# Delta rule's triangular inverse: 8x8 blocks and two doublings in place of 16x16 and one, with masks for selections

## The chip, the cores and the metric

The kernel runs on one core of a Trainium2 chip. The metric is the device time of one execution in microseconds (us). The core has five engines with instruction queues of their own, each run strictly in program order: PE (TensorE, matmul), DVE (VectorE), ACT (ScalarE), POOL (GpSimd) and SP (SyncE, which issues most transfers). They wait for one another by semaphores.

## The reference, cut to what matters

A hybrid decoder layer, 1024 tokens of width 1024. One projection feeds a gated delta rule (4 heads of 128) and a differential attention (4 heads); an output projection, then a gated feed-forward layer of 2816 follow. The change touches the delta rule alone. With chunks of tokens it solves a unit lower triangular system per chunk and head:

```
g = jnp.cumsum(chunks(g), axis=-1)
decay = jnp.exp(jnp.where(tril, g[..., :, None] - g[..., None, :], -jnp.inf))
lower = jnp.where(strict, jnp.einsum('bhnid,bhnjd->bhnij', k_beta, k) * decay, 0.0)
sol = lax.linalg.triangular_solve(eye + lower, rhs, left_side=True, lower=True,
                                  unit_diagonal=True)
...
v_new = value_i - jnp.einsum('bhck,bhkv->bhcv', kcd_i, state)      # scan over chunks
state = state * jnp.exp(gl_i)[..., None, None] + jnp.einsum('bhck,bhcv->bhkv', k_i, v_new)
```

The kernel takes chunks of 128 tokens, so there are NT = 8 chunks a head, and it works with the transposed system: `U` holds one 128x128 upper triangular matrix per chunk, side by side in a 128x1024 tile.

## The kernel before, in words

The program has four stretches: loading and normalising (to about 95 us), the four heads of the delta rule with the projections around them (95 to about 350 us), attention and the output projection (to about 760 us), and the feed-forward layer (to the end). The order of the instructions is fixed when the program is built: parts of the program have priorities (the table `PRI`, unchanged here), and a scheduler lays out each engine's queue by them. At run time no engine overtakes anything in its own queue.

In the delta stretch PE's queue is filled up with the matmuls of the projections: `gT` (L422 to L424, three matmuls of 128x512 for one product in split precision) and `pn` (L403 to L406). Between them stand the short matmuls of the heads. For head h the functions are:

- `delta_prep`: loads the cumulated decay as rows (`dec`), takes the exponential `eg`, subtracts the column term `Gc` (DVE L592), masks the triangle (POOL L594), and takes one exponential over 128x1024 (ACT L597). It runs a convolution of four taps for k, q and v (`conv4`: ACT L570, three DVE L573, silu ACT L575), transposes k, q and v on PE (`pk` L611, `pv` L657), and forms `pkk`, `pkq` (L638, L639), `U` (L643) and `dec` (L645).
- `delta_inverse`: cuts the four 32x32 diagonal blocks out of `U` into `Ud` (four POOL selections, L673), inverts their 16x16 diagonal blocks by 15 rounds of a DVE shuffle, multiply and subtract (L684, L685, L687), spreads the result into 32x32 blocks `Zd`, transposes it to `ZdT`, and doubles the block size once with two groups of 32 matmuls of 32x32 (`pv0` L696, `pz0` L702). Two further doublings, to 64 and to 128 (`pv1` L714, `pz` L726, `pv2` L736, `pz2` L741), follow.
- `delta_scan`: eight chunks in sequence, each a chain between PE and DVE: `pP` (PE L754), DVE L756, `pzz` (L758), DVE L762, `pS` (L766), DVE L771. It also evicts on ACT (L763, L776).
- `delta_out`: normalises and gates the output.

The inverse of head h+1 is laid out between the steps of the scan of head h on DVE, and the preparation of one head beside the inverse of the one before. POOL meanwhile also forms `wlo` (L204), the low part of projection weights, from two tiles in SBUF.

## Time and profile before

| | |
|---|---|
| median of 3 runs | 1429.08 us (1425.96 to 1431.47) |
| profiled execution | 1430.1 us, span 1428.4 us |
| PE busy | 1334.5 us, 93% of the span |
| DVE busy | 878.3 us, 61% |
| ACT busy | 611.3 us, 43% |
| POOL busy | 377.0 us, 26% |
| mean granted TensorE clock | 0.975 |

Busy is the time in which an engine had an instruction running; PE's can overlap its own next instruction. The chain of work that ended last consists almost only of PE instructions of the feed-forward layer.

### The profile page before, as it was taken

To read this page: it belongs to the slowest core of one execution; us is meant where nothing else is said; L and a number is where in the kernel's file an instruction comes from. 1 tells how busy PE (TensorE), PEld (TensorE's weight loads), DVE (VectorE), ACT (ScalarE), POOL (GpSimd) and SP (SyncE) were. 2 spreads that over 40 slices of the span, in tenths; PEclk is the share of its full clock that TensorE was granted. 3 is DMA by queue.
4 is the path that set the end of the run, shared out by engine and by line. 5 is a ranking of instruction groups with operands and counts; after the bars stand their busy time and mean duration, and the time that the engine had idled before them with its cause. 6 is when DMAs were issued, how large, how long until landed. Compare 5 with 4: busy or idle time off the path is not lost. (4 is left out here: it accounts for less than half of the span.)

```text
span 1428.4 us, 20608 instructions
## 1 busy us (share of the span) xinstructions
PE 1334.5 (93%) x7927; PEld 1126.6 (79%) x7927; DVE 878.3 (61%) x1745; ACT 611.3 (43%) x1086; POOL 377.0 (26%) x295
## 2 busy tenths in 40 slices
PE   7998898989989998999887999999999989999998
PEld 6876676888989986778665788888888868888887
DVE  5467978886342368867787666666666656334321
ACT  6445454533325365665554444444444435222220
POOL 3044313131242245240022434444333420000000
PEclk8999999999999999999998999999999999999999
DMA  7231112031543267455331222222222247547421
GB/s 225 83 80 35 34 39 75 17 113 66 162 109 116 88 169 192 105 134 162 123 121 29 89 74 89 85 78 89 89 74 82 82 137 243 195 149 229 139 88 59
DMA packets 143393, 155.14 MB, mean 109 GB/s; under 512 B 9279, under 2 KB 114367, under 8 KB 143295
## 3 DMA queue, kind: packets, MB, share of 16 engines
q1 hardware_dynamic: 130815, 144.14, 31.8%
q0 software_dynamic: 11008, 8.39, 3.1%
q8 instruction: 62, 1.02, 0.3%
q10 hardware_dynamic: 1472, 1.29, 0.3%
q14 instruction: 36, 0.29, 0.1%
HBM read 111.32 MB, written 38.29 MB: 105 GB/s over the span
## 5 line engine op out<-in xcount | busy, mean ns | idle before, releaser
L385 PE MATMUL pd<-whi,gl 128*128 128x512 f32 x352 | 137.0, 389 | 0.0
L383 PE MATMUL pd<-whi,gh 128*128 128x512 f32 x352 | 137.0, 389 | 0.0
L384 PE MATMUL pd<-wlo,gh 128*128 128x512 f32 x352 | 137.0, 389 | 0.0
L204 POOL TENSOR_TENSOR wlo<-raw,whi 128x1024 fp32r<-128x1024 f32 x34 | 83.8, 2471 | 194.1 <-PE gT L424 68.2
L1316 POOL TENSOR_TENSOR acc<-acc,acc 128x1024 f32<-128x1024 f32 x22 | 53.6, 2437 | 243.8 <-issue 215.5
L403 PE MATMUL pn<-whi,xn 128*128 128x256 f32 x448 | 116.3, 293 | 0.0
L404 PE MATMUL pn<-whi,xn 128*128 128x256 f32 x448 | 115.4, 291 | 0.0
L1339 ACT ACTIVATE gh<-act 128x1024 fp32r<-128x1024 f32 x42 | 44.6, 1061 | 123.9 <-PE pd L384 100.2
L1340 DVE TENSOR_TENSOR gl<-act,gh 128x1024 fp32r<-128x1024 f32 x42 | 52.0, 1241 | 68.9 <-ACT gh L1339 68.6
L403 PEld LDWEIGHTS pn<-whi,xn 128*128 128x128 f32 x448 | 87.3, 195 | 0.3
L404 PEld LDWEIGHTS pn<-whi,xn 128*128 128x128 f32 x448 | 87.0, 195 | 0.1
L202 ACT ACTIVATE whi<-raw 128x1024 fp32r<-128x1024 f32 x58 | 61.0, 1052 | 52.1 <-issue 18.3
L206 DVE TENSOR_TENSOR wlo<-rx,whi 128x1024 fp32r<-128x1024 f32 x22 | 28.9, 1315 | 82.6 <-ACT whi L202 82.3
L424 PE MATMUL gT<-xn,wlo 128*128 128x512 f32 x192 | 79.3, 413 | 0.0
L1230 PE MATMUL pa<-xT,whi 128*128 128x512 f32 x176 | 70.5, 400 | 9.3 <-ACT xT L1103 5.3
L422 PE MATMUL gT<-xn,whi 128*128 128x512 f32 x192 | 78.8, 410 | 0.0
L423 PE MATMUL gT<-xn,whi 128*128 128x512 f32 x192 | 78.6, 409 | 0.0
L202 ACT ACTIVATE whi<-rx 128x1024 fp32r<-128x1024 f32 x22 | 23.3, 1061 | 127.4 <-POOL rx L1271 127.4
L383 PEld LDWEIGHTS pd<-whi,gh 128*128 128x128 f32 x352 | 66.1, 188 | 13.8
L385 PEld LDWEIGHTS pd<-whi,gl 128*128 128x128 f32 x352 | 66.1, 188 | 13.7
L384 PEld LDWEIGHTS pd<-wlo,gh 128*128 128x128 f32 x352 | 66.1, 188 | 13.6
L206 DVE TENSOR_TENSOR wlo<-raw,whi 128x1024 fp32r<-128x1024 f32 x24 | 29.4, 1225 | 72.3 <-PE pd L384 53.1
(377 smaller groups left out, 3765.9 us busy)
## 6 DMA issues: line engine op xcount, KB each, us to landing
act<-act_dram SPq DMA_DIRECT2D x42, 512.0 KB, 4.5
rw<-in_w_up_dram SPq DMA_DIRECT2D x22, 512.0 KB, 3.8
act_dram<-acc SPq DMA_DIRECT2D x22, 512.0 KB, 2.6
raw<-in_w_down_dram SPq DMA_DIRECT2D x22, 512.0 KB, 4.4
raw<-in_w_in_dram SPq DMA_DIRECT2D x18, 512.0 KB, 4.0
pn_dram<-pn SPq DMA_DIRECT2D x16, 512.0 KB, 3.4
rx<-in_w_up_dram SPq DMA_DIRECT2D x22, 256.0 KB, 2.8
rz<-in_w_up_dram SPq DMA_DIRECT2D x22, 256.0 KB, 3.3
```

Source lines behind the costliest of these rows:

```text
L202: S.activation(hi, raw[:, 0:w], AF.Copy)
L204: G.tensor_tensor(lo, raw[:, 0:w], hi.bitcast(F32), op=ALU.subtract)
L206: V.tensor_tensor(lo, raw[:, 0:w], hi.bitcast(F32), op=ALU.subtract)
L383: PE.matmul(ps, lh, rh, start=first, stop=False)
L384: PE.matmul(ps, lh, rl, start=False, stop=False)
L385: PE.matmul(ps, ll, rh, start=False, stop=last)
L403: PE.matmul(o, xs(xn, 0, kt, a, b), wh, start=kt == 0, stop=False)
L404: PE.matmul(o, xs(xn, 1, kt, a, b), wh, start=False, stop=False)
L422: PE.matmul(o, whi[:, kt, :], xs(x_, 0, kt, *qs), start=kt == 0, stop=False)
L423: PE.matmul(o, whi[:, kt, :], xs(x_, 1, kt, *qs), start=False, stop=False)
L424: PE.matmul(o, wlo[:, kt, :], xs(x_, 0, kt, *qs), start=False, stop=kt == NK - 1)
L1230: PE.matmul(ps, wh[:, ks], xh[k], start=first, stop=False, skip_group_check=not start)
```

## The change

The diff does four things. (1) The column term of the decay goes into the exponential as its bias (`nGc`, the negated `Gc`): the subtraction over 128x1024 goes, and one exponential becomes eight of 128x128, since the bias is one column per chunk. (2) The diagonal 32x32 blocks are copied by ACT without a selection, and multiplied on DVE by constant masks (`s8`, `o8`, `o16`, `m8`), which come in a larger constant table. (3) The blocks that are inverted by rounds are 8x8: 7 rounds over narrower rows in place of 15. (4) From 8 to 16 and from 16 to 32 the pass with `pv0` and `pz0` runs, so twice a head; its first eviction moves from DVE to ACT. The attention mask leaves the early load of constants and is loaded by a transfer of its own.

```diff
--- before.py
+++ after.py
@@ -25,7 +25,9 @@
 NF = FFN // P
 EPS = 1e-6
 LAM_INIT = 0.8 - 0.6 * math.exp(-0.3 * 0)
-C_ID, C_TRI, C_MASK, C_ID16, C_FREQ, C_AB, C_W = 0, 128, 256, 384, 400, 408, 410
+
+C_ID, C_TRI, C_FREQ, C_ID8, C_M8, C_S8, C_O8, C_O16, C_W, C_MASK = 0, 128, 256, 264, 272, 276, 308, 340, 372, 372
+C_ALL = C_MASK + 128
 
 
 GB, WB, RB, LB, JB, CB, SB, OB, LA, S1, S2 = 16, 5, 3, 2, 2, 4, 8, 1, 2, 3, 5
@@ -44,13 +46,17 @@
 
 
 def constants():
-    c = np.zeros((P, C_W), np.float32)
+    c = np.zeros((P, C_ALL), np.float32)
     c[:, C_ID:C_ID + P] = np.eye(P)
     i = np.arange(P)
     c[:, C_TRI:C_TRI + P] = i[:, None] <= i[None, :]
     c[:, C_MASK:C_MASK + P] = np.where(i[None, :] <= i[:, None], 0.0, -1e30)
-    c[:, C_ID16:C_ID16 + 16] = (i % 16)[:, None] == np.arange(16)[None, :]
-    c[:, C_AB:C_AB + 2] = (i // 16 % 2)[:, None] == np.arange(2)[None, :]
+    r, j = (i % 32)[:, None], np.arange(32)[None, :]
+    c[:, C_ID8:C_ID8 + 8] = (i % 8)[:, None] == np.arange(8)[None, :]
+    c[:, C_M8:C_M8 + 4] = r // 8 == np.arange(4)[None, :]
+    c[:, C_S8:C_S8 + 32] = (r // 8 == j // 8) & (r < j)
+    c[:, C_O8:C_O8 + 32] = (r // 16 == j // 16) & (r // 8 < j // 8)
+    c[:, C_O16:C_O16 + 32] = r // 16 < j // 16
     c[:, C_FREQ:C_FREQ + 8] = 500000.0 ** (-np.arange(0, 16, 2) / 16.0)
     return c
 
@@ -150,8 +156,8 @@
     k_sb = cp.tile([P, C_W], F32, name="k_sb")
     ident = k_sb[:, C_ID:C_ID + P]
     tri = k_sb[:, C_TRI:C_TRI + P]
-    id16 = k_sb[:, C_ID16:C_ID16 + 16]
-    halfA, halfB = k_sb[:, C_AB:C_AB + 1], k_sb[:, C_AB + 1:C_AB + 2]
+    id8, m8 = k_sb[:, C_ID8:C_ID8 + 8], k_sb[:, C_M8:C_M8 + 4]
+    s8, o8, o16 = (k_sb[:, a:a + 32] for a in (C_S8, C_O8, C_O16))
 
     warm = small("warm", 1, 1)
     G.memset(warm, 1.0)
@@ -172,7 +178,7 @@
     w1row = gt("w1row")
     xt0 = [load_x(0)]
     nc.scalar.dma_start(w1row, norm1_w.broadcast_to([P, D]))
-    nc.scalar.dma_start(k_sb, cst)
+    nc.scalar.dma_start(k_sb, cst[:, 0:C_W])
     xt0.append(load_x(1))
 
 
@@ -374,7 +380,8 @@
     identb = cp.tile([P, P], BF16, name="identb")
     G.tensor_copy(identb, ident)
     maskb = cp.tile([P, P], BF16, name="maskb")
-    G.tensor_copy(maskb, k_sb[:, C_MASK:C_MASK + P])
+    nc.sync.dma_start(rowsA[:, 640:768], cst[:, C_MASK:C_MASK + P])
+    G.tensor_copy(maskb, rowsA[:, 640:768])
 
 
     dab = cp.tile([P, NT, 8], F32, name="dab")
@@ -544,6 +551,8 @@
     V.tensor_tensor(ekd, Gl, Gc, op=ALU.subtract)
     S.activation(ekd, ekd, AF.Exp)
     S.activation(egl, Gl, AF.Exp)
+    nGc = g32("nGc")
+    V.tensor_scalar(nGc, Gc, -1.0, None, op0=ALU.mult)
 
 
     lamp = tmp(128)
@@ -589,12 +598,12 @@
         with part("d_dec"):
             eg = gt("eg")
             S.activation(eg, dec, AF.Exp)
-            V.tensor_tensor(by_chunk(dec), by_chunk(dec),
-                            Gc[:, h, :].unsqueeze(2).broadcast_to([P, NT, P]), op=ALU.subtract)
             G.affine_select(out=by_chunk(dec), in_=by_chunk(dec),
                             pattern=[[0, NT], [1, P]], base=0, channel_multiplier=-1,
                             compare_op=ALU.is_ge, fill=-1e30)
-            S.activation(dec, dec, AF.Exp)
+            for c in range(NT):
+                cs = slice(c * P, (c + 1) * P)
+                S.activation(dec[:, cs], dec[:, cs], AF.Exp, bias=nGc[:, h, c:c + 1])
         with part("d_k"):
             kT = conv4(4 + h)
         with part("d_q"):
@@ -663,6 +672,7 @@
     def delta_inverse(d):
 
 
+
         inv1, inv2 = gt("inv1"), gt("inv2")
         w4 = [by_chunk(inv1[:, i * 256:(i + 1) * 256], 32) for i in range(4)]
         Ud, Zd, bc, ZdT = w4
@@ -670,38 +680,41 @@
         Uv = by_chunk(d["U"])
         for b in range(4):
             bs = slice(32 * b, 32 * b + 32)
-            G.affine_select(out=Ud[bs], in_=Uv[bs, :, bs],
-                            pattern=[[0, NT], [1, 32]], base=0, channel_multiplier=-1,
-                            compare_op=ALU.is_gt, fill=0.0)
-        U16, Z16, bc16 = (by_chunk(inv2[:, 512 + i * 128:640 + i * 128], 16) for i in range(3))
-        S.activation(U16, Ud[:, :, 0:16], AF.Copy, scale=halfA)
-        V.scalar_tensor_tensor(U16, Ud[:, :, 16:32], halfB, U16, op0=ALU.mult, op1=ALU.add)
-        G.memset(Ud[:, :, 0:16], 0.0)
-        G.tensor_scalar(Ud[:, :, 16:32], Ud[:, :, 16:32], halfA, None, op0=ALU.mult)
-        V.tensor_copy(Z16, id16.unsqueeze(1).broadcast_to([P, NT, 16]))
-        for l in range(15, 0, -1):
-            n = 16 - l
-            V.stream_shuffle(bc16[:, :, 0:n], Z16[:, :, l:16], [l] * 16 + [16 + l] * 16)
-            V.tensor_tensor(bc16[:, :, 0:n], bc16[:, :, 0:n], U16[:, :, l:l + 1].broadcast_to([P, NT, n]),
+            S.activation(Ud[bs], Uv[bs, :, bs], AF.Copy)
+        by_c = lambda m: m.unsqueeze(1).broadcast_to([P, NT, 32])
+        Uo = by_chunk(inv2[:, 512:768], 32)
+        U8, Z8, bc8 = (by_chunk(inv2[:, 768 + i * 64:832 + i * 64], 8) for i in range(3))
+        V.tensor_tensor(bc, Ud, by_c(s8), op=ALU.mult)
+        V.tensor_reduce(U8, bc.rearrange("p c (s j) -> p c j s", j=8), axis=AX.X, op=ALU.add)
+        V.tensor_copy(Z8, id8.unsqueeze(1).broadcast_to([P, NT, 8]))
+        for l in range(7, 0, -1):
+            n = 8 - l
+            V.stream_shuffle(bc8[:, :, 0:n], Z8[:, :, l:8], [8 * (i // 8) + l for i in range(32)])
+            V.tensor_tensor(bc8[:, :, 0:n], bc8[:, :, 0:n], U8[:, :, l:l + 1].broadcast_to([P, NT, n]),
                             op=ALU.mult)
-            V.tensor_tensor(Z16[:, :, l:16], Z16[:, :, l:16], bc16[:, :, 0:n], op=ALU.subtract)
-        S.activation(Zd[:, :, 0:16], Z16, AF.Copy, scale=halfA)
-        V.tensor_scalar(Zd[:, :, 16:32], Z16, halfB, None, op0=ALU.mult)
+            V.tensor_tensor(Z8[:, :, l:8], Z8[:, :, l:8], bc8[:, :, 0:n], op=ALU.subtract)
+        V.tensor_tensor(Zd.rearrange("p c (s j) -> p c s j", j=8),
+                        Z8.unsqueeze(2).broadcast_to([P, NT, 4, 8]),
+                        m8.unsqueeze(1).unsqueeze(3).broadcast_to([P, NT, 4, 8]), op=ALU.mult)
         V.transpose(inv1[:, 768:1024], inv1[:, 256:512])
-
-        pv0 = psS("pv0")
-        for c in range(NT):
-            for b in range(4):
-                bs = slice(32 * b, 32 * b + 32)
-                PE.matmul(pv0[bs, c * 32:c * 32 + 32], Ud[bs, c, :], ZdT[bs, c, :], start=True, stop=True)
-        V.tensor_copy(inv1[:, 512:768], pv0[:, 0:256])
-        pz0 = psS("pz0")
-        for c in range(NT):
-            for b in range(4):
-                bs = slice(32 * b, 32 * b + 32)
-                PE.matmul(pz0[bs, c * 32:c * 32 + 32], bc[bs, c, :], Zd[bs, c, :], start=True, stop=True)
-        V.tensor_tensor(inv1[:, 256:512], inv1[:, 256:512], pz0[:, 0:256], op=ALU.subtract)
-        V.transpose(inv1[:, 768:1024], inv1[:, 256:512])
+        V.tensor_tensor(Uo, Ud, by_c(o8), op=ALU.mult)
+
+        for off in (Uo, Ud):
+            pv0 = psS("pv0")
+            for c in range(NT):
+                for b in range(4):
+                    bs = slice(32 * b, 32 * b + 32)
+                    PE.matmul(pv0[bs, c * 32:c * 32 + 32], off[bs, c, :], ZdT[bs, c, :], start=True, stop=True)
+            S.activation(inv1[:, 512:768], pv0[:, 0:256], AF.Copy)
+            if off is Uo:
+                V.tensor_tensor(Ud, Ud, by_c(o16), op=ALU.mult)
+            pz0 = psS("pz0")
+            for c in range(NT):
+                for b in range(4):
+                    bs = slice(32 * b, 32 * b + 32)
+                    PE.matmul(pz0[bs, c * 32:c * 32 + 32], bc[bs, c, :], Zd[bs, c, :], start=True, stop=True)
+            V.tensor_tensor(inv1[:, 256:512], inv1[:, 256:512], pz0[:, 0:256], op=ALU.subtract)
+            V.transpose(inv1[:, 768:1024], inv1[:, 256:512])
         G.memset(ZT[0:32, :, 32:64], 0.0)
         G.tensor_copy(ZT[0:32, :, 0:32], ZdT[0:32])
         G.tensor_copy(ZT[32:64, :, 32:64], ZdT[32:64])
```

The lines of the changed kernel are shifted: the rounds are L692, L693, L695, `pv0` is L707, `pz0` L715, the transposes `pk` are L620, the convolution is L582 and the silu L584.

DVE's queue, head 0's inverse (tile `inv`) and the convolutions of k and q of head 1 (`acc_1432`, `acc_1438`), before:

```order
L687 TENSOR_TENSOR inv_143_1045<-inv_143_1045 128x8x4
L592 TENSOR_TENSOR dec_1246<-dec_1246,Gc 128x1024
L573 SCALAR_TENSOR_TENSOR acc_1432<-pT_1248,dcw,acc_1432 128x1023
L573 SCALAR_TENSOR_TENSOR acc_1438<-pT_1307,dcw,acc_1438 128x1023
L573 SCALAR_TENSOR_TENSOR acc_1432<-pT_1248,dcw,acc_1432 128x1022
L573 SCALAR_TENSOR_TENSOR acc_1438<-pT_1307,dcw,acc_1438 128x1022
L573 SCALAR_TENSOR_TENSOR acc_1432<-pT_1248,dcw,acc_1432 128x1021
L573 SCALAR_TENSOR_TENSOR acc_1438<-pT_1307,dcw,acc_1438 128x1021
L684 STREAM_SHUFFLE inv_143_1045<-inv_143_1045 128x8x5
```

and with the change (`acc_1491` and `acc_1497` are the same convolutions):

```order
L692 STREAM_SHUFFLE inv_143_1054<-inv_143_1054 128x8x5
...
L695 TENSOR_TENSOR inv_143_1054<-inv_143_1054 128x8x5
L692 STREAM_SHUFFLE inv_143_1054<-inv_143_1054 128x8x6
...
L695 TENSOR_TENSOR inv_143_1054<-inv_143_1054 128x8x6
L692 STREAM_SHUFFLE inv_143_1054<-inv_143_1054 128x8x7
L693 TENSOR_TENSOR inv_143_1054<-inv_143_1054 128x8x7
L695 TENSOR_TENSOR inv_143_1054<-inv_143_1054 128x8x7
L696 TENSOR_TENSOR inv_142_1053<-inv_143_1054,k_sb 128x256
L582 SCALAR_TENSOR_TENSOR acc_1491<-pT_1301,dcw,acc_1491 128x1023
L582 SCALAR_TENSOR_TENSOR acc_1497<-pT_1360,dcw,acc_1497 128x1023
L582 SCALAR_TENSOR_TENSOR acc_1491<-pT_1301,dcw,acc_1491 128x1022
```

All seven rounds and the multiply by `m8` (L696) now stand ahead of the convolutions; before, four rounds and the subtraction L592 did.

PE's queue at the transposes of k of head 1, before (`gT` are projection matmuls):

```order
L423 MATMUL gT_1972<-xn_141,whi_1942 128x512
L611 MATMUL pk_1447<-k_sb,acc_1432 128x128 x4
L611 MATMUL pk_1457<-k_sb,acc_1432 128x128 x4
L424 MATMUL gT_1972<-xn_140,wlo_1943 128x512
...
L422 MATMUL gT_1972<-xn_140,whi_1942 128x512
L611 MATMUL pk_1467<-k_sb,acc_1438 128x128 x4
...
L611 MATMUL pk_1476<-k_sb,acc_1438 128x128 x4
```

and with the change:

```order
L429 MATMUL gT_2075<-xn_140,whi_2045 128x512
L707 MATMUL pv_144_1086<-inv_142_1053,inv_143_1054 32x32 x27
L620 MATMUL pk_1506<-k_sb,acc_1491 128x128 x4
L620 MATMUL pk_1516<-k_sb,acc_1491 128x128 x4
L707 MATMUL pv_144_1086<-inv_142_1053,inv_143_1054 32x32 x5
L430 MATMUL gT_2075<-xn_141,whi_2045 128x512
...
L620 MATMUL pk_1526<-k_sb,acc_1497 128x128 x4
L715 MATMUL pz_145_1121<-inv_142_1053 32x32 x9
L620 MATMUL pk_1535<-k_sb,acc_1497 128x128 x4
```

Head 0's first doubling now stands on both sides of these transposes; 27 of its 32 matmuls are ahead of them. Between `pv` of head 0 and these transposes there are 57 `gT` matmuls, where there were 51.

PE's queue at the second doubling of head 0, which the kernel before has not; `pv_1605` and `pv_1611` are the transposes of v of head 1:

```order
L431 MATMUL gT_2134<-xn_140,wlo_2105 128x512
L666 MATMUL pv_1605<-k_sb,acc_1599 128x128 x2
L707 MATMUL pv_146_1156<-inv_142_1053 32x32 x32
L666 MATMUL pv_1605<-k_sb,acc_1599 128x128 x2
L666 MATMUL pv_1611<-k_sb,acc_1599 128x128 x2
L715 MATMUL pz_147_1190<-inv_142_1053 32x32 x4
L666 MATMUL pv_1611<-k_sb,acc_1599 128x128
L715 MATMUL pz_147_1190<-inv_142_1053 32x32
L666 MATMUL pv_1611<-k_sb,acc_1599 128x128
L715 MATMUL pz_147_1190<-inv_142_1053 32x32 x27
L429 MATMUL gT_2134<-xn_140,whi_2104 128x512
```

Before, the two groups of 32 of the only pass stood at this place with three `gT` matmuls and more between them; now there are four 128x128 transposes.

## Rows read from the trace of the kernel before

**Rows 1.** windows: busy us of each engine (x instructions), TensorE clock, DMA share, GB/s

```profile
95.00:350.00 255.00, 224.47 (x2145) 188.79 (x2144) 209.77 (x585) 117.09 (x284) 70.96 (x57) 0.96 0.17 53
760.00:1430.00 670.00, 654.52 (x2856) 536.98 (x2856) 365.32 (x373) 245.57 (x262) 157.38 (x104) 0.99 0.35 112
125.00:150.00 25.00, 20.00 (x92) 16.11 (x91) 23.65 (x60) 14.26 (x30) 10.95 (x10) 0.96 0.12 37
150.00:175.00 25.00, 21.56 (x262) 17.09 (x261) 23.09 (x82) 8.93 (x28) 10.46 (x11) 0.98 0.09 23
```

**Rows 2.** waits of PE, 95 to 350 us: total, times, longest

```profile
PE pk L611 <- ACT acc L575: 8.3, 2, 5.1
PE pzz L758 <- DVE s L756: 5.3, 3, 2.1
PE pS L766 <- DVE s L762: 4.0, 4, 1.7
PE pkq L639 <- DVE dec L645: 3.2, 2, 1.7
PE pP L754 <- DVE s L771: 3.1, 2, 1.6
PE pv L657 <- ACT acc L575: 3.0, 2, 1.8
```

**Rows 3.** groups on DVE, 95 to 360 us: busy, mean ns, idle before

```profile
L687 DVE TENSOR_TENSOR inv<-inv 128x8 f32<-128x8 f32 (+14 forms) x60 | 20.9, 348 | 1.2
L685 DVE TENSOR_TENSOR inv<-inv 128x8 f32<-128x8 f32 (+14 forms) x60 | 17.6, 294 | 1.5
L684 DVE STREAM_SHUFFLE inv<-inv 128x8 f32<-128x8 f32 (+14 forms) x60 | 14.2, 236 | 0.0
...
L592 DVE TENSOR_TENSOR dec<-dec,Gc 128x1024 f32<-128x1024 f32 x4 | 4.9, 1220 | 8.9 <-ACT eg L591 8.9
...
L703 DVE TENSOR_TENSOR inv<-inv,pz 128x256 f32<-128x256 f32 x4 | 1.7, 414 | 0.0
```

**Rows 4.** groups on POOL, 95 to 360 us

```profile
L673 POOL TENSOR_SCALAR_AFFINE_SELECT inv<-U 32x256 f32<-32x256 f32 x16 | 14.8, 923 | 0.7
```

**Rows 5.** timeline of DVE at 264.9 us: start, length

```profile
264.94 2.33 DVE L687 TENSOR_TENSOR inv<-inv 128x120 f32<-128x120 f32 x1
```

**Rows 6.** timeline of POOL at the same place

```profile
264.73 2.40 POOL L204 TENSOR_TENSOR wlo<-raw,whi 128x1024 fp32r<-128x1024 f32 x1 [9.01 <-PE gT L423]
```

**Rows 7.** timeline of PE around the first block of 32x32 matmuls

```profile
169.03 0.40 PE L422 MATMUL gT<-xn,whi 128*128 128x512 f32 x1
169.26 0.39 PE L423 MATMUL gT<-xn,whi 128*128 128x512 f32 x1
169.73 0.75 PE L696 MATMUL pv<-inv 32*32 32x32 f32 x64
170.41 0.50 PE L424 MATMUL gT<-xn,wlo 128*128 128x512 f32 x1
```

**Rows 8.** timeline of ACT before the first head's values

```profile
129.58 0.40 ACT L677 ACTIVATE inv<-inv,k_sb 128x128 f32<-128x128 f32 x1 [9.04 <-POOL inv L673]
129.89 1.04 ACT L575 ACTIVATE acc<-acc 128x1024 f32<-128x1024 f32 x1
```

**Rows 9.** timeline of DVE around the second head's convolutions

```profile
134.23 1.22 DVE L592 TENSOR_TENSOR dec<-dec,Gc 128x1024 f32<-128x1024 f32 x1
135.37 10.23 DVE L573 SCALAR_TENSOR_TENSOR acc<-pT,dcw,acc 128x1023 f32<-128x1023 f32 x6
```

**Rows 10.** windows around a pair of PE waits, columns as in rows 1

```profile
240.80:246.80 6.00, 2.52 (x12) 1.55 (x11) 5.71 (x18) 2.77 (x4) 5.17 (x6) 1.00 0.11 38
246.80:250.20 3.40, 3.40 (x17) 3.12 (x16) 2.20 (x13) 0.73 (x2) 0.00 (x0) 0.50 0.58 154
```

**Rows 11.** groups on ACT, 95 to 360 us

```profile
L763 ACT ACTIVATE s<-pzz,cj 128x128 f32<-128x128 f32 x28 | 10.1, 361 | 31.0 <-DVE s L762 30.4 <-PE pzz L758 0.6
L718 ACT ACTIVATE U<-inv 32x256 f32<-32x256 f32 x16 | 6.6, 414 | 6.4 <-DVE inv L685 4.2 <-DVE inv L703 2.0
```


## The prediction

> **What bounds the kernel now.** I read the busy time by stretch first. The feed-forward stretch is PE's: 654.5 of 670 us, clock 0.99, and the change does not reach it [rows 1]. Attention isn't touched either, apart from a mask that arrives long before it is used. So the change can only act between 95 and 350 us. There PE is busy for 224.5 of 255 us, which leaves 30.5 us of idle time, and DVE is busy for 209.8. In two windows DVE has hardly a gap, 23.65 and 23.09 of 25 us, while PE stands 5.0 and 3.4 us [rows 1]. The second view is what PE waits for there [rows 2]. The six groups sum to 26.7 us, and all but the first head's 5.1 us for its silu depend on DVE's or ACT's queue in the heads. The stretch is therefore PE work with holes that DVE's queue makes: time is saved by closing holes, and lost by giving PE more to do. Since the projection matmuls that fill PE have to run anyway, each us added to PE's work or to its holes moves the end by about one us.
>
> A third view shows how some holes arise. A multiply and subtract of a round takes about 0.3 us, but this one takes 2.33 us [rows 5], and POOL's subtraction over two tiles in SBUF runs from 264.73 to 267.13 [rows 6]: the DVE instruction ends when POOL's does. The scan's L762 stands behind it, PE's pS behind that, and this is the 1.7 us in the group of pS. The three waits of pzz (5.3 us) and the two of pP (3.1 us) [rows 2] look the same in the timeline: a copy or a round's multiply of about 2 us under POOL work, five times. Such collisions make 5.3 + 3.1 + 1.7 = 10.1 us of the holes.
> The Trainium skill says so too (Trainium Architecture — The Big Picture, "What this means for kernel authors"): DVE and GpSimd share a port pair by an exclusive lock. By that rule the new mask multiplies, with two SBUF inputs each, are as exposed as the rounds were; that is the fourth case below.
>
> **The change part by part.**
>
> *Work on DVE.* A round costs 0.348 + 0.294 + 0.236 = 0.88 us on the mean [rows 3], so eight fewer are 7.0 us a head. The subtraction gives back 1.22 us [rows 3], the eviction and the small merging instructions about 1 us. Added are four multiplies over 128x256, one reduction of that size to 128x64, one more subtraction and one more transpose: seven at about 0.41 us, the price of L703, which has the same shape [rows 3], makes 2.9 us. Net: about -6.3 us a head, -25 us in all, of 209.8. POOL loses its 16 selections, 14.8 us [rows 4]. ACT gains, per head, four copies of 0.41 and two evictions like them, and eight exponentials of 0.36 each, 2.9 us, in place of a single one over the same elements [rows 11]; it was busy for 117 of 255 us, so I cost this at nothing. What covers it is ACT's idle time; where an exponential stands before an eviction of the scan it can hold it by 0.36 us.
>
> *PE's own work: +6.8 us.* A block of 32 matmuls of 32x32 is 64 records in 0.75 us [rows 7]. From L423 at 169.26 to the next gT at 170.41 are 1.15 us where two neighbours are 0.23 apart, so it displaces 0.92 us. Two more blocks a head are eight: 6.0 us by the block, 7.4 by the displacement. I take 6.8.
> The Trainium skill (TensorE: Matmul & The Clock Gate, "Back-to-back issue gap") gives for such short matmuls a floor of about 25 ns, or about 62 ns where the sequencer decodes each in software. By 62 ns the 256 matmuls would cost 15.9 us and the sum below would come out 9 us higher; the row, 0.75 us for 32, is 23 ns each, and it decides.
>
> *Waiting inside the second pass: +1.0 us.* pz0 needs pv0's eviction and pv1 a subtraction and a transpose. Before, three gT matmuls (0.7 us) and more cover each step. Now the four 128x128 transposes of v, or four short pn, cover the second eviction: about 0.55 us against an eviction of 0.41 (as L718) [rows 11] and the handing over. I take 0.25 us a head; bounds 0 and 0.6 a head, 2.4.
>
> *First head's values: -0.7 us.* ACT's queue stands 9.04 us for POOL's selections, and the silu behind it starts at 129.89 [rows 8]. Without them it starts when the convolution ends, by the timeline about 0.7 us earlier, and pv's 1.8 us [rows 2] shrinks by that. Bounds 0 and -1.8.
>
> *k of head 1: +1.3 us.* PE's wait there is 8.3 - 5.1 = 3.2 us [rows 2]. The convolutions start at 135.37, right behind L592 [rows 9]. With the change, all the rounds and four mask multiplies are ahead of them: three more rounds (2.1 us, being narrow), four multiplies and a reduction (2.0 us), less L592 (1.22), less a merge and its wait (0.8). They start about 2.1 us later. Against that, six convolution steps take 10.23 us [rows 9] with POOL's selection and a wlo over them, and part of this goes. PE arrives later as well, by six gT at 0.23 less the 0.7 won just before: 0.7 us. The 27 matmuls of pv0 ahead of pk wait for a transpose that stands behind the convolutions, but are through when the silu of k is. The wait grows by 0.6 to 1.9 us.
>
> *Preparation of head 1: -1.5 us.* Eleven rounds that stood among its steps on DVE are gone. Two waits, 1.7 us in the group of pkq and 3.0 - 1.8 = 1.2 us in that of pv beyond the first head's [rows 2], hang on that queue; I take a bit over half. Bounds 0 and -2.9.
>
> *Collisions: -5 us of 10.1.* Of the five in pzz and pP and the one in pS, three hit rounds 12, 13 and 15, which no longer exist (the largest is rows 5). The others hit a copy or a round that stays. Per head the DVE instructions between SBUF tiles in the inverse fall from 33 to some 21, but wlo also moves on POOL, whose selections no longer hold it up. By the count a third goes, 3.4 us; at best all. I take half.
>
> *Other waits of the scans: -1.7 us.* pS waits 4.0 - 1.7 = 2.3 us beyond that collision, 0.7 of it behind L592. I take 0.7 and 1.0 of the rest.
>
> *Clock: -1.7 us.* Behind two close waits (PE busy for 2.52 of 6 us) the granted clock is 0.50, the 1.2 GHz level, for 3.4 us [rows 10]. That costs 1.7 us each time. Behind the k of head 1 it falls too, as it will again; of the two falls in the scans I count one gone.
>
> *Sum:* 6.8 + 1.0 - 0.7 + 1.3 - 1.5 - 5.0 - 1.7 - 1.7 = -1.5 us. From the profiled 1430.1 us this gives 1428.6. The median of the runs lies 1.0 us below that profiled execution, so the forecast is **1427.5 us**. The best ends of all terms (6.0 for PE, no wait in the second pass, all collisions and clock falls gone) give about -14 us; the worst (7.4, 2.4, 1.9 and no relief) about +12 us.
>
> **The rivals.** 0.5%, 7.1 us, is about what a measurement of this kernel tells from no change.
>
> *Holes close (faster).* DVE loses 12% of its work in the stretch, and the holes come from a queue that is nearly full, so most vanish together: -9 for collisions, -2.9, -3.4 for the clock, -2.3 for pS, -0.7, against 6.8 + 0.6: -11 us, 1418 us. For it: DVE at 23 of 25 us where PE waits. Against it: each hole is a single late instruction, not a queue that never catches up, as PE's full windows between them show.
>
> *PE pays, relief fails at k (slower).* The convolutions of head 1 slip by more than the 2.1 us counted: the decay's selection no longer waits for a subtraction and falls on the rounds ahead of them, and one multiply of about 2 us is added. The wait of pk becomes about 7 us (+3.9), and each later step of head 1 starts as late; with 6.8 + 1.0 and only 3.4 of relief the sum is +8 us, 1437 us. It decides from about 5 us of growth at this place, or when relief stays under 1 us. For it: the queue rows of DVE.
>
> *The masks collide as the rounds did.* The holes stay in number and size: 6.8 + 1.0 + 1.3 - 0.7 - 1.5 - 1.7 = +5 us, 1434 us, within 0.5%.
>
> **How the numbers follow.** Forecast as summed 0.40 (its own range 1421 to 1434); holes close 0.29; pays at k 0.18; masks collide 0.13. The forecast case leaves a little on either side: faster by over 0.5% 0.33, within 0.5% 0.45, slower 0.22. The range reaches from the middle of the faster case's lower half to just past the slower case: 1415 to 1439 us.
>
> **What the profile after would show.** PE's busy time in the delta stretch up by 6 to 7.5 us, with 256 more matmuls of 32x32; DVE's down by about 25 us, POOL's by about 15 to 18. PE's wait for k of head 1 near 4.5 us. Waits of pzz, pP and pS below 10 us together; if they are above 14, the collision term is wrong, if under 3, the faster case holds. The second pz0 of each head waiting for ACT by under 0.6 us; over 1 us there, the eviction's place in ACT's queue was misjudged. The feed-forward stretch must have the same length; if it has not, the cause lies outside this reading.

## The result: slower by 1.2%

The changed kernel takes 1445.02 us (median of 4 runs, 1441.69 to 1451.49) against 1427.52 us of the kernel before on the same chips: a ratio over the executions of 1.0118, 95% interval 1.0088 to 1.0148 (the medians alone give 1.0123). That lies above the forecast range of 1415 to 1439 us. The profiled execution has a span of 1442.4 us.

First, where the time came. The first matmul of attention's scores starts at 410.8 us before and at 426.0 us with the change, 15.2 us later, and what follows it is as long as before (1017.6 and 1016.4 us). Of the 15.2 us, 0.9 are there already ahead of the delta stretch: the short matmuls `pg` (the sums of the decay), which stand in front of it, start at 85.45 us before and at 86.34 with the change. The rest lies where the change was made. A window from 95 us to that matmul, of the kernel before (busy us of PE, PEld, DVE, ACT and POOL with their instructions, then the granted clock, DMA share, GB/s):

```profile
95.00:410.80 315.80, 284.41 (x2623) 246.73 (x2622) 230.10 (x646) 138.08 (x323) 89.49 (x72) 0.97 0.24 72
```

and of the changed kernel, with the stretches of [rows 1]:

```profile
95.00:426.00 331.00, 302.71 (x3138) 259.24 (x3137) 209.83 (x530) 150.91 (x367) 70.46 (x48) 0.95 0.23 69
95.00:350.00 255.00, 228.58 (x2479) 188.48 (x2478) 183.73 (x462) 128.65 (x326) 51.23 (x31) 0.94 0.16 48
760.00:1430.00 670.00, 651.41 (x2846) 534.53 (x2846) 372.24 (x383) 252.15 (x272) 164.76 (x109) 0.99 0.34 109
```

DVE fell by 26.0 us between 95 and 350 us (209.8 to 183.7), and POOL by 19.7. But the changed kernel has done less of its work by 350 us; over the same work, up to attention, DVE fell by 20.3 us (230.1 to 209.8) and POOL by 19.0. PE's idle time up to attention fell too, from 315.8 - 284.4 = 31.4 to 331.0 - 302.7 = 28.3 us. But PE's busy time rose by 18.3 us where 6.8 was expected. Busy time contains the clock: the parts of it that ran at a granted clock of 0.50 (1.2 GHz) are 17.4 us before and 29.7 us after, and half of that is lost time, 8.7 and 14.8 us, if the same work takes twice as long at that clock (an estimate). What is left is PE's work at the full clock: 275.7 and 287.9 us. So the 15.2 us are 12.2 of work, 6.1 of clock and -3.1 of idle time. This split is the measure for every experiment below; I call its parts idle, clock and work.

At 95 us the two kernels are not equally far, so the work is counted from the first `pg` as well:

```profile
85.45:410.79 325.34, 293.95 (x2666) 254.61 (x2665) 232.40 (x651) 142.08 (x330) 91.88 (x73) 0.97 0.25 73
86.34:426.04 339.70, 311.41 (x3178) 266.43 (x3177) 212.25 (x536) 154.96 (x374) 72.90 (x49) 0.95 0.24 70
```

By these the work is 293.95 - 8.7 = 285.3 and 311.41 - 14.8 = 296.6 us, 11.3 more. Idle and clock are the same from either start.

The waits of PE in the changed kernel (us in total, times, longest), 95 to 365 us, to be held against [rows 2]:

```profile
PE omT L814 <- DVE acc L808: 5.4, 3, 3.6
PE pk L620 <- ACT acc L584: 4.4, 1, 4.4
PE pv L666 <- ACT acc L584: 3.4, 2, 2.2
PE pS L779 <- DVE s L775: 3.4, 2, 2.5
PE pv L707 <- DVE inv L699: 3.0, 1, 3.0
PE pkq L648 <- DVE dec L654: 1.8, 1, 1.8
PE pzz L771 <- DVE U L756: 1.2, 1, 1.2
...
PE pz L715 <- ACT inv L708: 0.6, 1, 0.6
```

The collisions in the scans went away as hoped: pzz from 5.3 to 1.2, pP from 4.4 (3.1 and 1.3) to nothing. The 3.0 us of pv0 take the place of the second head's wait for k, since 27 matmuls of pv0 stand ahead of it. New are the waits of omT, the transposes of the gated output (5.4 us), and a longer one of pv. On DVE, 95 to 370 us, as in [rows 3]:

```profile
L695 DVE TENSOR_TENSOR inv<-inv 128x8 f32<-128x8 f32 (+6 forms) x28 | 10.3, 369 | 0.6
...
L693 DVE TENSOR_TENSOR inv<-inv 128x8 f32<-128x8 f32 (+6 forms) x28 | 8.7, 311 | 0.7
...
L692 DVE STREAM_SHUFFLE inv<-inv 128x8 f32<-128x8 f32 (+6 forms) x28 | 5.7, 203 | 0.0
...
L716 DVE TENSOR_TENSOR inv<-inv,pz 128x256 f32<-128x256 f32 x8 | 3.3, 414 | 1.7 <-PE pz L715 1.7
...
L688 DVE TENSOR_REDUCE inv<-inv 128x64 f32<-128x256 f32 x4 | 2.5, 620 | 0.0
...
L687 DVE TENSOR_TENSOR inv<-inv,k_sb 128x256 f32<-128x256 f32 x4 | 1.6, 410 | 0.0
```

The masks (L687) and the subtraction (L716) cost 0.41 us as estimated, the reduction 0.62.

**How PE's work grew.** PE in the last head's second pass (start, length, instructions, idle time before):

```profile
336.96 0.75 PE L707 MATMUL pv<-inv 32*32 32x32 f32 x64 [0.17 <-DVE inv L717]
...
338.94 0.26 PE L715 MATMUL pz<-inv 32*32 32x32 f32 x6 [0.56 <-ACT inv L708]
342.79 0.48 PE L814 MATMUL omT<-k_sb,acc 128*128 128x128 f32 x1 [3.60 <-DVE acc L808]
343.20 0.33 PE L715 MATMUL pz<-inv 32*32 32x32 f32 x8
343.46 0.47 PE L814 MATMUL omT<-k_sb,acc 128*128 128x128 f32 x1
343.86 0.42 PE L715 MATMUL pz<-inv 32*32 32x32 f32 x10
```

After pv0, PE waits 0.56 us for ACT's eviction and then 3.60 us for omT, because the scheduler has put the 8 transposes of the gated output between the pieces of pz0. From there, 8 to 10 records of 32x32 and one transpose alternate, each at twice the length or more that it has in a group. Part of that is the clock, which is at its lower level from 341.85 us on (the test strip below tells the two apart):

```profile
336.30:341.80 5.50, 2.17 (x79) 1.60 (x77) 5.33 (x9) 1.82 (x4) 4.66 (x2) 1.00 0.06 16
341.90:352.00 10.10, 9.21 (x92) 6.97 (x93) 4.68 (x14) 2.73 (x6) 0.78 (x2) 0.50 0.21 86
```

In the 5.5 us ahead of the fall PE was busy for 2.17. The wait itself is a collision once more, at a new place. DVE's and POOL's timelines there:

```profile
336.83 1.94 DVE L191 TENSOR_TENSOR rto<-rto,ms 128x8 f32<-128x8 f32 x1
338.81 2.26 DVE L192 SCALAR_TENSOR_TENSOR ro<-rto,ro 128x8 f32<-128x8 f32 x1
...
341.30 0.17 DVE L191 TENSOR_TENSOR rto<-rto,ms 128x8 f32<-128x8 f32 x1
...
342.38 0.88 DVE L808 SCALAR_TENSOR_TENSOR acc<-acc,ro,szh 128x128 f32<-128x128 f32 x3
```

```profile
336.38 4.66 POOL L804 TENSOR_TENSOR szh<-szh,dnw 128x1024 f32<-128x1024 f32 x2 [9.87 <-ACT szh L803]
```

Two instructions of 128x8 elements, which take 0.17 us a little later, take 1.94 and 2.26 us while POOL multiplies two SBUF tiles (4.66 us for two); the gating L808 starts at 342.38.

### The profile page after: what moved, and what is told of

The parts are those of the page before. It is cut to its first block, busy times and chain, and to the rows that moved or that the text cites. A ratio compares the mean times of both kernels' runs of the same rounds, so it can differ in the third digit from the quotient of the medians.

```text
span 1442.4 us, 21544 instructions
## 1 busy us (share of the span) xinstructions
PE 1351.2 (94%) x8439; PEld 1137.5 (79%) x8439; DVE 858.7 (60%) x1630; ACT 624.5 (43%) x1130; POOL 357.0 (25%) x271
## 3 DMA queue, kind: packets, MB, share of 16 engines
q1 hardware_dynamic: 130959, 144.21, 31.4%
## 5 line engine op out<-in xcount | busy, mean ns | idle before, releaser
L208 ACT ACTIVATE whi<-raw 128x1024 fp32r<-128x1024 f32 x58 | 61.0, 1052 | 50.3 <-issue 18.3
L391 PEld LDWEIGHTS pd<-wlo,gh 128*128 128x128 f32 x352 | 66.1, 188 | 13.7
L392 PEld LDWEIGHTS pd<-whi,gl 128*128 128x128 f32 x352 | 66.1, 188 | 13.6
L413 PE MATMUL pn<-wlo,xn 128*128 128x256 f32 x448 | 71.5, 293 | 2.0 <-POOL wlo L210 2.0
```

The source lines that it names most:

```text
L208: S.activation(hi, raw[:, 0:w], AF.Copy)
L391: PE.matmul(ps, lh, rl, start=False, stop=False)
L392: PE.matmul(ps, ll, rh, start=False, stop=last)
L413: PE.matmul(o, xs(xn, 0, kt, a, b), wf(kt)[1], start=False, stop=kt == NK - 1)
```

## The experiments

Sixteen kernels ran. Each edit stands as a short diff against the kernel named in its expectation. The table has what was measured: the ratio to the kernel before with its 95% interval, and the parts from 95 us to attention's first score matmul, in us. "From pg" is the work counted from the first `pg`, which starts between 83.4 and 88.3 us in these kernels, so that all but the second pass is the same work in all of them (out_later has 17 short projection matmuls more in it, about 2 us, and three others 2 or 3). "Changes" counts, in PE's instructions from there to attention, the places at which a 32x32 matmul stands next to one of a larger tile. mix_cost, the test strip, is the kernel before up to there.

| kernel | ratio (95%) | idle | clock | work | from pg | changes |
|---|---|---|---|---|---|---|
| before | 1 | 31.4 | 8.7 | 275.7 | 285.3 | 46 |
| mix_cost | | 30.9 | 5.9 | 279.4 | 286.2 | 46 |
| changed | 1.0118 (1.0088, 1.0148) | 28.3 | 14.8 | 287.9 | 296.6 | 120 |
| one_pass | 1.0003 (0.9991, 1.0014) | 25.4 | 15.0 | 276.1 | 284.9 | 52 |
| two_passes | 1.0172 (1.0155, 1.0189) | 35.1 | 15.4 | 285.4 | 296.3 | 90 |
| seven_rounds | 0.9998 (0.9980, 1.0016) | 31.4 | 9.4 | 274.9 | 285.5 | 52 |
| bias_alone | 1.0020 (1.0000, 1.0041) | 30.6 | 11.3 | 274.8 | 286.0 | 46 |
| masks_no_bias | 1.0006 (0.9983, 1.0029) | 31.0 | 10.6 | 274.6 | 284.7 | 46 |
| masks_16 | 0.9946 (0.9929, 0.9963) | 26.0 | 10.3 | 272.7 | 284.2 | 44 |
| masks_16_dve | 0.9938 (0.9917, 0.9959) | 25.3 | 7.7 | 274.6 | 285.6 | 46 |
| before_inv_earlier | 1.0015 (0.9998, 1.0031) | 33.1 | 8.6 | 275.1 | 285.8 | 46 |
| inv_earlier | 1.0102 (1.0082, 1.0121) | 34.9 | 11.7 | 282.3 | 292.4 | 74 |
| inv_a_little | 1.0052 (1.0032, 1.0073) | 27.1 | 13.6 | 283.9 | 293.0 | 84 |
| out_later | 1.0094 (1.0064, 1.0123) | 30.3 | 14.2 | 284.9 | 295.1 | 78 |
| omt_later | 1.0040 (1.0018, 1.0062) | 28.7 | 12.7 | 282.8 | 293.3 | 74 |
| evict_dve | 1.0016 (1.0002, 1.0030) | 26.3 | 10.0 | 284.3 | 294.7 | 96 |
| evict_dve_inv | 1.0115 (1.0093, 1.0138) | 36.4 | 16.7 | 280.4 | 291.6 | 74 |
| evict_dve_omt | 1.0102 (1.0070, 1.0135) | 33.5 | 19.8 | 279.8 | 290.9 | 70 |

The ratios are over several executions, the parts of the one that was profiled; for bias_alone that one took 1428.19 us where the median is 1433.04. before and mix_cost show what parts of one queue differ by: 3 us of clock, 1 of work from pg. The nine rows with one pass all have 284.2 to 286.2 us of work from pg, so this column is the firm one; differences of 3 us in the clock column are not.

**Is it the second pass?** (one_pass, two_passes)

```diff
 one_pass, of the changed kernel
-        for off in (Uo, Ud):
+        for off in (Uo,):
 two_passes, of the kernel before: pv0, eviction, pz0, subtraction, transpose
+        for _ in range(2):
```

> The changed kernel without its second doubling (the pass from 16 to 32 is left out, so the blocks stay incomplete). Theory A, the second pass is what costs: its 32x32 matmuls, their mixing with 128x128 transposes on PE and the falls of the clock behind it make about 17 us, and the relief on DVE is worth a few us; 1422 to 1428 us. Theory B, the pass costs only the 6.8 us of its matmuls and the rest lies in the order around the convolutions of k of the second head: 1436 to 1440 us.

> The kernel before with its one doubling pass run a second time on the same blocks (the result is spoilt; nothing else changes). Theory A, a pass costs 10 us or more where pz0 stands between the transposes omT (it does in heads 1 to 3 here, 4 or 5 pieces): 1437 to 1444 us. Theory B, a pass costs the time of its block of matmuls, 6.8 us, and a little for the wait: 1434 to 1436 us.

Without the second pass the changed kernel takes 1426.98 us, the time of the kernel before; with a second pass the kernel before takes 1451.95 us, 25 us more. Theory A holds for one_pass; two_passes lies above both ranges, on A's side. The pass is the loss; the convolutions of the second head, which my slower rival blamed, are not. The split is more exact: from one_pass to the changed kernel work grows by 11.8 us (11.7 from pg), idle by 2.9, and the clock part stays (15.0 and 14.8). So the pass costs by PE's work above all. What the rest of the change won in idle time against the kernel before, 6.0 us, the clock had already taken back in one_pass, 6.3 us.

**What were the rounds and the selections worth?** (seven_rounds, bias_alone, masks_no_bias, masks_16, masks_16_dve)

```diff
 seven_rounds, of the kernel before
-        for l in range(15, 0, -1):
+        for l in range(15, 8, -1):
 bias_alone, of the kernel before: eight exponentials with bias=nGc, no subtraction
 masks_16, of the changed kernel
+        V.tensor_tensor(bc, Ud, by_c(s16), op=ALU.mult)
+        V.tensor_tensor(U16, bc[:, :, 0:16], bc[:, :, 16:32], op=ALU.add)
...
+        for l in range(15, 0, -1):
 masks_no_bias, of masks_16: subtraction and one exponential as before
 masks_16_dve, of masks_16
-        S.activation(inv1[:, 512:768], pv0[:, 0:256], AF.Copy)
+        V.tensor_copy(inv1[:, 512:768], pv0[:, 0:256])
```

> The kernel before with rounds 8 to 15 of the inverse left out (the result is spoilt). Theory A, the rounds lay beside PE's work, and without them the order of the convolutions of the next head moves behind the inverse: 1424 to 1430 us. Theory B, DVE's rounds bind the delta stretch, as its 23 of 25 busy us suggest: 1412 to 1420 us.

> The kernel before with the column term as bias of eight exponentials and the mask's separate load; nothing of the inverse is changed. Theory A, bias and masks each give part of the 7 us that both gave with 16x16 blocks: 1421 to 1425 us. Theory B, the gain is that of the selections taken from POOL alone: 1426 to 1429 us.

> The kernel with 16x16 blocks, masks and one doubling, but with the subtraction on DVE and the single exponential of before in place of the bias. Theory A, the masks alone make the gain of 7 us, since the bias alone made none: 1418 to 1423 us. Theory B, the bias is needed to free DVE for the masks: 1425 to 1429 us.

> The changed kernel with 16x16 blocks, 15 rounds and one doubling as before, but with the bias, the ACT copies and the masks. Theory A, masks and bias are a small gain and the second pass is the loss: 1420 to 1427 us. Theory B, the masks on DVE and the copies and exponentials on ACT cost what the selections on POOL did not: 1432 to 1440 us.

> The fastest kernel so far (16x16 blocks, masks and bias, one doubling) with the eviction of pv0 on DVE. Theory A, DVE's place for the eviction is shorter for the chain of the pass: 1415 to 1419 us. Theory B, with one pass and 15 rounds on DVE it only loads the fuller engine: 1420 to 1427 us.

Leaving out eight rounds gains nothing: 0.9998 (0.9980 to 1.0016), as theory A said. Idle time is 31.4 us as before, with other names on it. PE's waits in seven_rounds, 95 to 350 us:

```profile
PE pS L766 <- DVE s L762: 5.1, 4, 1.8
PE pz L702 <- DVE inv L697: 3.4, 1, 3.4
PE pzz L758 <- DVE s L756: 2.7, 2, 1.7
...
PE po L775 <- ACT s L763: 2.5, 3, 2.1
```

pzz fell from 5.3 to 2.7 us, but pS rose, and pz0 and po, which hardly waited before, wait for 3.4 and 2.5. With both the masks and the bias at 16x16 blocks the kernel takes 1419.34 us and beats both kernels by 0.54% and more, 0.7 us below theory A's range; neither half does it alone. For masks_no_bias the rival was right (1428.68), and bias_alone (1433.04) lies above both ranges. Idle time falls by 5 us only where both are there. Evicting on DVE changes nothing there beyond the intervals (1419.63, between the two ranges). Since masks_16 differs from one_pass mainly by the blocks, 8x8 blocks are not even a gain before the second pass is paid for: 1419 against 1427 us on the same chip.

**What makes the pass dear: mixing?** (mix_cost)

```diff
 mix_cost, of the kernel before, behind the last result; four(c): 4 matmuls 32x32, one(c): a transpose
+        for _ in range(4):
+            for c in range(NT):
+                four(c)
+            for c in range(NT):
+                one(c)
+            for c in range(NT):
+                four(c)
+                one(c)
```

> The kernel before with a test strip behind the end of its work: four times 32 matmuls of 32x32 together, 8 transposes of 128x128 together, and the same 32 and 8 once more, four to one in turn. Theory A, changing between the two shapes costs PE time: the mixed form takes about 1.3 to 1.8 us longer at the full clock than the sum of the two groups (about 0.75 and 1.1 us). Theory B, the order is free: the same within 0.2 us, and the longer stretches in the changed kernel come from the clock or from waits.

PE in the strip, second repetition:

```profile
1427.63 0.75 PE L1369 MATMUL pzm<-fres 32*32 32x32 f32 x64
1428.32 1.09 PE L1372 MATMUL om<-k_sb,fres 128*128 128x128 f32 x8
1429.34 0.26 PE L1369 MATMUL pzm<-fres 32*32 32x32 f32 x8
1429.53 0.33 PE L1372 MATMUL om<-k_sb,fres 128*128 128x128 f32 x1
1429.79 0.26 PE L1369 MATMUL pzm<-fres 32*32 32x32 f32 x8
1429.98 0.33 PE L1372 MATMUL om<-k_sb,fres 128*128 128x128 f32 x1
...
1432.70 0.33 PE L1372 MATMUL om<-k_sb,fres 128*128 128x128 f32 x1
1432.96 0.75 PE L1369 MATMUL pzm<-fres 32*32 32x32 f32 x64
```

The two groups take 1429.34 - 1427.63 = 1.71 us, the same instructions in turn 1432.96 - 1429.34 = 3.62 us. Nothing waits in either. The mixed form has 14 changes of shape more. So mixing costs 1.9 us, about 0.14 us for each of them: theory A, a little above its range. The kernels bear it out: over the nine with two passes, work from pg rises with the count of changes, from 290.9 us at 70 to 296.6 at 120, by about 0.11 us a change (a straight line through them, the extra projection matmuls taken off; single kernels lie up to 2 us beside it). The windows of the strip give the clock too:

```profile
1422.10:1427.60 5.50, 5.50 (x146) 3.83 (x144) 0.69 (x1) 0.00 (x0) 0.00 (x0) 1.00 0.27 98
1427.63:1429.34 1.71, 1.71 (x74) 1.50 (x73) 0.00 (x0) 0.00 (x0) 0.00 (x0) 1.00 0.05 10
1429.34:1432.96 3.62, 3.62 (x73) 2.33 (x72) 0.00 (x0) 0.00 (x0) 0.00 (x0) 1.00 0.00 0
...
1434.67:1438.30 3.63, 3.63 (x74) 2.33 (x73) 0.00 (x0) 0.00 (x0) 0.00 (x0) 1.00 0.00 0
1438.30:1441.60 3.30, 3.30 (x82) 2.84 (x81) 0.00 (x0) 0.00 (x0) 0.00 (x0) 0.51 0.02 5
```

PE has work all the time, and still the granted clock drops to 0.51, behind 16 us of such short matmuls, for one stretch of 3.3 us.

**Does keeping the group together give it back?** (inv_earlier, inv_a_little, out_later, omt_later; control before_inv_earlier)

```diff
 PRI, of the changed kernel (before_inv_earlier: the same of the kernel before)
-dinv=200, dout=100
+dinv=300, dout=100      inv_earlier
+dinv=250, dout=100      inv_a_little
+dinv=200, dout=0        out_later
 omt_later: the transposes omT and their evictions in a part of their own
+        with part("omt"):     # omt=-150
```

> The changed kernel with one number of the priority table changed (dinv 300 for 200), after which the second group of 32 matmuls of the second pass stands together in heads 1, 2 and 3 and no longer between the transposes omT. Theory A, mixing and waiting for the gated output cost some 2 us of PE and some 2 us of clock a head: 1432 to 1438 us. Theory B, mixing costs nothing and the matmuls themselves are dear: 1443 to 1447 us.

> A control: the kernel before with the priority of the inverse raised as in the run with the second group together (dinv 300 for 200), the work unchanged. Theory A, the layout of the same work moves the time by less than 4 us, and the differences of 15 us belong to the second pass: 1424 to 1431 us. Theory B, layout alone moves it as much as the whole change: outside 1420 to 1436 us.

> The changed kernel with another number of the priority table (dout 0 for 100), which also keeps the second pass's second group of matmuls together in heads 1, 2 and 3, but by moving the gated output back instead of the inverse forward. Theory A, mixing costs about 5 us of PE's work in the stretch and the gated output's wait another 3 to 5: 1433 to 1440 us, with PE's work at full rate before attention at about 282 us, as with the inverse moved forward, against 287.9. Theory B, the work of 282 us there came from something else: it stays at 286 to 289 us.

> The changed kernel with dinv 250 for 200: the second group stands together in heads 1 and 2 and stays between the transposes in the last head. Theory A, each head mixed costs about 2 us of PE's work and the last head's wait and clock fall another 8: 1439 to 1443 us. Theory B, the layout decides and a small step of priority can move the time by 10 us: below 1436 or above 1446 us.

> The changed kernel with the transposes omT and their evictions alone moved back in priority (a part of their own, 150 below the gated output), so that the second pass's pz0 stands together in heads 1, 2 and 3, and PE does not wait for the gated output inside the pass. Theory A, mixing and that wait inside the second pass are most of the 17 us: 1430 to 1437 us. Theory B, the chain through the second pass stands exposed wherever the transposes are: 1439 to 1446 us.

PE's work falls in all four edits of the changed kernel, to 282.3 to 284.9 us (from pg to 292.4 to 295.1, against 296.6), as it must if mixing costs PE's time; out_later, at 284.9, lies between its two theories there. But the time follows only in omt_later (1435.55 us, as theory A said) and inv_a_little (1435.89, below theory A's range and 0.1 us inside theory B's). inv_earlier (1442.21) lies between its two ranges, and out_later (1441.35) above theory A's. In inv_earlier the waits took back what the work gave, 95 to 430 us:

```profile
PE omT L814 <- DVE acc L808: 4.8, 3, 3.8
...
PE pv L666 <- ACT acc L584: 4.3, 2, 3.1
PE pz L715 <- ACT inv L708: 3.4, 1, 3.4
...
PE pzz L771 <- DVE U L756: 3.2, 1, 3.2
```

The last head's second pass now waits 3.4 us for its eviction, which stands in ACT's queue behind a silu that waits for its load; the transposes of v wait for 4.3 us (3.1 of them in head 1) and one scan step for 3.2. Moving the inverse in the kernel before, with its single pass, moves the time by 0.15% (1432.13 us, 1.1 above theory A's range). The same number moves the changed kernel no more, from 1.0118 to 1.0102; other edits of its order move that one by up to 1%. Whether the kernel before is less delicate is not shown: one edit of its order alone was tried.

**Is it the engine that evicts?** (evict_dve, evict_dve_inv, evict_dve_omt)

```diff
-            S.activation(inv1[:, 512:768], pv0[:, 0:256], AF.Copy)
+            V.tensor_copy(inv1[:, 512:768], pv0[:, 0:256])
```

> The changed kernel with the eviction of pv0 on DVE, as before the change, in place of ACT. Theory A, the second pass costs by PE's work, mixing and clock, whichever engine evicts: 1441 to 1447 us. Theory B, the eviction behind ACT's queue is what makes the pass long: 1430 to 1436 us.

> The changed kernel with both edits that were tried apart, the eviction of pv0 on DVE and the inverse moved forward. Theory A, mixing costs PE time that this saves in heads 1 and 2: 1424 to 1429 us, work at full rate before attention about 282 us. Theory B, the two edits get in each other's way as layouts do: 1431 to 1440 us.

> The same with the eviction of pv0 on DVE. Theory A: 1424 to 1430 us, since the only mixing left there was with omT. Theory B, what the eviction on DVE won was a lucky layout: 1433 to 1445 us.

With the eviction on DVE the changed kernel takes 1430.23 us, 0.16% above the kernel before. I had expected no effect, and theory B seemed right. But its combinations with the two earlier edits are back at 1.0115 (1445.13 us, above both ranges) and 1.0102 (1443.78, as theory B said), while having the least work of all kernels with two passes (280.4 and 279.8 us). So the engine alone isn't the cause: the same edit gains 1% on one order, nothing on two others (inv_earlier, masks_16) and loses 0.6% on omt_later. It changes PE's order too (96 changes of shape instead of 120), and with it come other idle and clock parts; how the one brings the other is not shown. In evict_dve the last head's 22 us from 330 on have PE busy for 21.62 at clock 1.00; in evict_dve_omt PE waits for the gated output once more, 95 to 430 us:

```profile
PE omT L815 <- DVE acc L808: 9.7, 2, 4.9
```

and its clock part is the largest of the table.

## Why the prediction was wrong

The sum was -1.5 us, and 15.2 were measured: it missed by 16.7. By the parts, PE's work was forecast at +6.8 and came to +11.3, the waits at -6.6 and came to -3.1, the clock at -1.7 and came to +6.1, and 0.9 us arose ahead of the stretch, where executions of one queue differ by more (`pg` starts at 85.45 us in the kernel before and at 88.23 in mix_cost). one_pass divides it another way. Without the second pass the forecast's terms make -1.5 - 6.8 - 1.0 = -9.3 us, and one_pass measured no change; the pass itself was forecast at 7.8 us and costs 14.4 from pg to attention (339.7 against 325.3). So two steps failed, in like measure: the relief, which was counted as kept, and the price of the pass on PE.

*Bound, and DVE's relief: a step that failed, by its worth.* The attention and feed-forward stretches kept their lengths, as forecast. DVE lost 20 us over the same work against 25 forecast, POOL 19. (The six groups of PE's waits sum to 26.9 us, not 26.7; nothing hangs on it.) The collisions in pzz, pP and pS went from 10.1 us to a single hold of 2.5; I had halved them. But I took the gain of each closed hole as kept. seven_rounds shows that it is not: holes that close reappear further on. The idle part fell by 3.1 us in all, where my terms for waits summed to -6.6. In one_pass it fell by 6.0, and the clock part rose by 6.3: there the holes closed about as forecast, and the time did not follow.

*PE's own work: the other step that failed.* The price of a block, 0.75 us for 32 matmuls, holds in a group: the two-pass kernels that keep most groups together have 6 to 10 us more work from pg than the kernel before, and one_pass, without the pass, has 284.9 us, as before. In the change it was 11.3 us more. I quoted the rows in which pz0 stands between 128x128 transposes and counted the transposes as cover for the wait; that they lengthen each other was not costed. The strip gives 1.9 us for it in a head that is mixed like the strip.

*Clock: the wrong sign.* I counted one fall fewer (-1.7 us). There were more and longer ones, 29.7 busy us at half clock against 17.4, so +6.1; of single executions, which for one queue differ by 3. The falls of the last two heads, 6.8 and 10.2 us long, come right behind second passes in which PE waited or ran short mixed matmuls (busy for 4.11 and 2.17 of the 5.5 us ahead). The pass is not their only cause, since one_pass loses as much, with a fall of 10.2 us near 328. Over all executions, the median of the mean granted clock is 0.977 for the kernel before (beside one_pass), 0.972 for one_pass and 0.969 for the changed kernel.

*Waiting inside the second pass.* For the eviction itself 0.6 us was measured, 1.0 forecast. The wait that mattered, 3.60 us in the last head and 5.4 in all, is for the gated output that had been laid into the pass; I had not looked at what else stands there.

*k of head 1: near, by luck.* PE's wait there is the 3.0 us ahead of pv0; 3.2 before, and about 4.5 were forecast. The convolutions start at 139.62 instead of 135.37, 2 us more than I said, since one round's multiply was held for 2.10 us under a wlo:

```profile
136.13 2.10 DVE L693 TENSOR_TENSOR inv<-inv 128x48 f32<-128x48 f32 x1
...
139.62 7.25 DVE L582 SCALAR_TENSOR_TENSOR acc<-pT,dcw,acc 128x1023 f32<-128x1023 f32 x6
```

They take 7.25 instead of 10.23 us, though, and pk starts at 148.17, 1.3 us later than before. This bears out the slower rival's collision but not its price: that the time came out on that rival's side, above its 1437 us, had another cause.

*First head's values and preparation of head 1.* pv starts at 130.18, 0.8 us earlier; 0.7 was forecast. Of head 1's two waits, 1.7 us for pkq went, and that for v grew from 1.3 to 2.2 us; -1.5 was forecast.

*What stays open.* Shown is that the second pass makes the loss, that it adds 11.7 us to PE's work, some 6 for its matmuls by the block's price and so 5 to 6 for mixing, and that eight rounds of DVE's work, left out of the kernel before, bring no time. Not settled is what sets idle and clock in a given layout. Seven edits that leave PE the same matmuls spread the 8x8 kernel from 1430 to 1445 us; out_later, evict_dve_inv and evict_dve_omt, all above 1441 us, have single falls of 13.7 to 20.5 us, but so has omt_later, 17.1 us, which is among the better ones. No run here sets these parts alone. Why bias and masks help only together is not settled either.

## What to carry to other kernels

Where an engine is filled to the brim with independent work, taking load off its neighbours is worth little until a run with that load left out shows otherwise; here eight rounds of DVE work were worth nothing. Added work on the full engine can cost more than its busy time (here 11.7 us of PE's work against 6.0 by the block): cost it with what the scheduler puts between its pieces, and look at those neighbours, not only at the piece. Test a change's parts by themselves: two of its four parts together (masks and bias at 16x16 blocks) gain 0.5%, which the smaller blocks and the second pass hid.

## What the runs showed of the hardware

Alternating four 32x32 matmuls with one 128x128 transpose costs about 0.14 us per change of shape: 3.62 us for what takes 1.71 in two groups, without a wait. The granted clock can fall to 0.5 (1.2 GHz) without any wait on PE, as it did behind 16 us of such short matmuls in the strip. It can also stay there for long while PE is fully busy; in out_later it fell behind 7.3 us in which PE was busy for 5.55, and stayed for the 17 us from 221.4 on:

```profile
214.00:221.30 7.30, 5.55 (x116) 3.77 (x116) 6.96 (x21) 4.19 (x8) 3.17 (x3) 1.00 0.02 5
221.40:238.40 17.00, 17.00 (x118) 13.15 (x118) 5.73 (x12) 6.32 (x34) 0.00 (x0) 0.50 0.27 94
```

The falls also differ between executions of one kernel, and the time with them: omt_later's ten go from 1425.07 us at a mean granted clock of 0.983 to 1439.22 at 0.970. And the hold of DVE under POOL work doesn't scale with DVE's size: instructions of 128x8 elements took 1.94 and 2.26 us instead of 0.17. They ended where POOL's two multiplies did, as the 128x120 elements of [rows 5] did, in 2.33 us.
